# Two attention heads per step, W_out chunk by chunk with the router work between, and a slot table that a permutation turns

## The chip, the cores and the metric

One core of one Trainium2 chip. The core has five engines with queues of their own: TensorE (PE in the profile; PEld is its weight load), VectorE (DVE), ScalarE (ACT), GpSimd (POOL) and SyncE (SP), which here only issues transfers. The metric is the device time of one execution in microseconds (us). All times below are from the kernel before.

## The reference, cut to what matters

One layer of an encoder on 512 tokens of width 1024, all in fp32:

```
P    = h @ W_in                        # q, k, v of A, B, C and three gates
A    = windowed attention, 8 heads of 64, 2 kv heads, band of 128, ALiBi, sink logit
B    = differential attention, 4 heads, each softmax1 - lambda*softmax2, RMS norm
C    = 2-D neighbourhood attention, 8 heads of 64, relative bias
mix  = W_out( sum_i sigmoid(gate_i) * (branch_i @ W_branch_i) )
x    = LN(alpha*x + mix)
x    = LN(alpha*x + MoE(x))            # top-4 of 32 experts, clamped SwiGLU, softmax router
```

## The kernel before

Tokens lie in four chunks of 128. A product that has to be exact to fp32 is made of three in a faster form: a weight is split into a high part (a rounded copy by ScalarE) and a low part (VectorE subtracts), and the products are hi·hi, lo·hi and hi·lo. Rows such as L129 to L131 (projections) or L783 to L785 (W_out) are such triples.

*Attention* (until about 480 us). `scores` (L198) makes the scores of one head u and one block of 128 queries with two products: L203 takes all 128 rows of the array (the head's 64 channels with high and low part of the query stacked), L204 takes 64 rows (high query by low key), rows 0 to 63 for u = 0 and 64 to 127 for u = 1. They are evicted to VectorE's `soft` (L207; the reduction is L210), with two PSUM buffers `sc`. `banded` (L230; A and C) does one head after the other: four query blocks, then per key block transposes, a split of the transposed probabilities (ph, pl) and `pv3`, three products with 64 output columns (L226 vh·ph, L227 vl·ph, L228 vh·pl). `evac_o` (L273) writes the head's output as high and low part. Between the steps a filler (`Fill.run`) puts the projections of the next heads and the branch gates, so that the triples L129 to L131 stand between attention's products. The scheduler of the framework then settles each engine's order.

*Gates of the third branch* (480 to 546 us), a pure run of products. *W_out with LN1 and the router* (546 to 643 us): `out_product` for chunks 0 to 2 together, k by k as the eight blocks of W_out arrive; then `layer_norm1` for each, which makes the router's logits, the top four (mx, mf) and the mask M; then the products of chunk 3 with the three layer_norm1 on the other engines; then chunk 3's. After that the counts per expert (L816, L818), each token's place in its expert (pos, L821, L822), the first expert's rows by one-hot products (L835, eight per chunk, 64 instructions in the profile), `finish1` for the four chunks (L767, L768, writes of X1 and Y), `sort` of the experts by load.

*MoE* (643 us to the end): 32 experts in an order in which expert 0 is always first (it needs no `order`) and the rest are sorted by load; KINDS says which place is large (L, split weights, 128 slots) or small (S, plain fp32). A weight block is 1 MB; 8 up and 4 down blocks per expert. Eight raw buffers (rawu, rawv) hold the stream; SyncE asks for a block (L610 up, L615 down) when its buffer is free. The slot table T in DRAM, whose column is the expert's place in the order, is filled by 16 indirect DMAs of GpSimd (L933, one per chunk and top-k rank), read back by three (L938, L939) and gives the rows to gather (tbs, tbl). `pick` (L1019, a GpSimd copy) spreads an expert's column of the sorted selector for the bias product L1095. The up products are L1084 (large) and L1102 (small), the bias of a large expert is L1079 (64 rows, alternating row halves).

Of the kernel before, what the change touches and what calls it, by code (L numbers as in the profile page):

```python
# [43 lines left out]
def kernel_body(ctx, tc, a, out, dbg=None, cap=128):  # L44
# [56 lines left out]
    for k in range(8):  # L101
        t = att.tile([P, NB, P], F32, name="E", bufs=7) if k < 7 else att.tile([P, NB, P], F32, name="t", bufs=3)
# [66 lines left out]
    def make_v(w, permuted, box):  # L169
# [8 lines left out]
        vh = att.tile([P, NB, P], F32R, name="vh", bufs=2)  # L178
        vl = att.tile([P, NB, P], F32R, name="vl", bufs=2)
# [3 lines left out]
        nc.scalar.copy(vh, pt)  # L183
        nc.vector.tensor_sub(vl, pt, vh.bitcast(F32))
        box["v"] = (vh, vl)
# [12 lines left out]
    def scores(box, u, qb, ks, ke):  # L198
        q2, (k2, kl) = box["q"], box["k"]
        r = slice(u * 64, u * 64 + 64)  # L200
        qs = slice(qb * P, qb * P + P)
        ps = ps_s.tile([P, S], F32, name="sc")
        nc.tensor.matmul(ps[:, :ke - ks], q2[:, u, qs], k2[:, u, ks:ke], start=True, stop=False)  # L203
        nc.tensor.matmul(ps[:, :ke - ks], q2[r, u, qs], kl[r, ks:ke], start=False, stop=True)  # L204
        return ps[:, :ke - ks]

    def soft(ps, bias, n, init, mcol, scol):  # L207
# [3 lines left out]
        e = att.tile([P, S], F32, name="E", bufs=7)  # L211
# [18 lines left out]
    def banded(box, u, biasf, init, sinkc, done):  # L230
        vh, vl = box["v"]
        vc = slice(u * 64, u * 64 + 64)
        m = att.tile([P, NB], F32, name="m", bufs=4)
        s = att.tile([P, NB], F32, name="s", bufs=4)
        es = []
        for qb in range(NB):
            ks, ke = rng(qb)
            ps = scores(box, u, qb, ks, ke)
            es.append(soft(ps, biasf(qb), ke - ks, init, m[:, qb:qb + 1], s[:, qb:qb + 1]))
            yield  # L240
        if sinkc is not None:
            sk = att.tile([P, NB], F32, name="sk", bufs=2)
            nc.scalar.activation(sk, m, AF.Exp, bias=sinkc)
            nc.vector.tensor_add(s, s, sk)
        r = att.tile([P, NB], F32, name="r", bufs=4)
        nc.vector.reciprocal(r, s)
        for qb in range(NB):
            ks, ke = rng(qb)
            nc.vector.tensor_scalar(es[qb][:, :ke - ks], es[qb][:, :ke - ks], r[:, qb:qb + 1], None,
                                    op0=ALU.mult)  # L250
        yield
        po = ps_o.tile([P, S], F32, name="o")
        pend = None
        for i, kb in enumerate((1, 2, 0, 3)):
            qs = [qb for qb in range(NB) if abs(qb - kb) <= 1]
            pt = ps_t.tile([P, S], F32, name="pt")
            n = len(qs) * P
            for j, qb in enumerate(qs):
                c0 = kb * P - rng(qb)[0]
                nc.tensor.transpose(pt[:, j * P:(j + 1) * P], es[qb][:, c0:c0 + P], ident)  # L260
            ph, pl = split_pt(pt, n)
            if pend:
                pv3(*pend)
            pend = (po[:64, qs[0] * P:qs[0] * P + n], n, ph, pl, vh[:, kb, vc], vl[:, kb, vc], i == 0, i == 3)
            yield
        pv3(*pend)
        done(po[:64])
        yield
# [4 lines left out]
    def evac_o(po, br, half, permuted):  # L273
        bh, bl = br
        r = slice(half * 64, half * 64 + 64)
        hi, hf, lo, src = bh[r], bh[r].bitcast(F32), bl[r], po
        if permuted:
            hi, hf, lo = perm(hi), perm(hf), perm(lo)
            src = out4(src)
        if half == 0:  # L280
            nc.scalar.copy(hi, src)
            nc.vector.tensor_sub(lo, src, hf)
        else:
            t = att.tile([P, S], F32, name="w", bufs=4)
            tt = out4(t[r]) if permuted else t[r]
            nc.scalar.copy(tt, src)
            nc.scalar.copy(hi, tt)
            nc.vector.tensor_sub(lo, tt, hf)
# [10 lines left out]
    def att_a(p, box):  # L299
        for u in range(2):  # L300
            h = p + 4 * u
            bt = att.tile([P, 896], F32, name="bias", bufs=2)
            (dma if p == 0 else nc.scalar.dma_start)(bt[:, :384], abv[:, h])

            def bf(qb):
                o = 128 if qb == 0 else 0
                ks, ke = rng(qb)
                return bt[:, o:o + ke - ks]
            yield from banded(box, u, bf, nsink[:, h:h + 1], sink[:, h:h + 1],
                              lambda po: evac_o(po, br_of(brA, h // 2), h % 2, False))  # L310

    def att_b(h, box):
        bt = att.tile([P, 896], F32, name="bias", bufs=2)
        nc.scalar.dma_start(bt, btv[:, h])
        vh, vl = box["v"]
# [10 lines left out]
        for qb in range(NB):  # L326
# [3 lines left out]
            ee = []  # L330
            for u in range(2):
                ps = scores(box, u, qb, 0, S)
                ee.append(soft(ps, bt[:, o:o + S], S, BIG, m[:, u:u + 1], s[:, u:u + 1]))
# [8 lines left out]
        for kb in range(NB):  # L342
# [6 lines left out]
            pend = (po, S, ph, pl, vh[:, kb], vl[:, kb], kb == 0, kb == 3)  # L349
# [30 lines left out]
    def att_c(p, box):  # L380
# [23 lines left out]
    def ph2_items(i, brs, db):  # L404
# [12 lines left out]
        def load():  # L417
# [4 lines left out]
            if pre_hook and db % 2:  # L422
                pre_hook[0](last[0])
# [32 lines left out]
    def qkv(kind, i):  # L456
        box = boxes.setdefault((kind, i), {})
        if kind == "A":
# [6 lines left out]
                (win(o + 1024 + i * P), lambda w: make_v(w, pm, box), 5.6)]  # L465
# [45 lines left out]
    T = dram.tile([P * E, 2], I32, name="T")  # L511
# [76 lines left out]
    wsp[0] = sW.enter_context(tc.tile_pool(name="wsp", bufs=2))  # L588
    nraw = [0]
# [9 lines left out]
    experts = {0: slice(0, 1)}  # L599

    def expert(p):

        if p not in experts:
            experts[p] = bass.ds(nc.values_load(order[0:1, p:p + 1], engines=[mybir.EngineType.SP], min_val=0,
                                                max_val=E - 1), 1)
        return experts[p]

    def up_raw(p, k):
        raw = raw_tile()
        dma(raw, a["w_up"][expert(p), k * P:(k + 1) * P, :].rearrange("o p c -> (o p) c"))  # L610
        return raw

    def down_raw(p, t):
        raw = raw_tile()
        dma(raw.rearrange("p (k d) -> p k d", k=2),  # L615
            a["w_down"][expert(p), t * 256:(t + 1) * 256, :].rearrange("o (k p) d -> p (o k) d", p=P))
# [10 lines left out]

    pre_hook.append(lambda ins: prefetch(ins, NRA))
    fill.add([ph2_items(2, brC, db) for db in range(8)])
    while fill.cur or fill.loaded or fill.items:  # L630
# [18 lines left out]
    nc.gpsimd.iota(iota, pattern=[[1, P]], base=0, channel_multiplier=0, allow_small_or_imprecise_dtypes=True)  # L649
    gt = moe.tile([3 * E, NB, P], F32R, name="gt")  # L650
    id16 = moe.tile([P, P], F16, name="id16")
    nc.gpsimd.tensor_copy(id16, ident)
# [10 lines left out]
    nc.gpsimd.iota(pcol, pattern=[[0, 1]], base=0, channel_multiplier=1, allow_small_or_imprecise_dtypes=True)  # L663
    half = moe.tile([P, 1], F32, name="half")
    nc.gpsimd.tensor_scalar(half, pcol, 64.0, None, op0=ALU.is_ge)
    iot2 = moe.tile([P, 2, 64], F32, name="iot2")
    nc.gpsimd.iota(iot2, pattern=[[0, 2], [1, 64]], base=1, channel_multiplier=0,
                   allow_small_or_imprecise_dtypes=True)
    rop = moe.tile([E, E], F32, name="rop")
    kw = dict(channel_multiplier=0, allow_small_or_imprecise_dtypes=True)  # L670
    ranks = dict(L=0, S=NL)
    for p, kind in enumerate(KINDS):
        nc.gpsimd.memset(rop[:, p:p + 1], float(ranks[kind]))
        ranks[kind] += 1
    sel0 = moe.tile([P, 1], F32R, name="sel0")
    for i in range(4):
        nc.gpsimd.tensor_copy(sel0[i * E:(i + 1) * E], ident[0:E, 0:1])
    sel = moe.tile([P, 2, E], F32R, name="sel")
    nc.gpsimd.memset(sel.bitcast(F32), 0.0)
    bu = moe.tile([P, 2, S], F32R, name="bu")  # L680

    s3 = ExitStack()
    sO = ExitStack()
    po_ = sO.enter_context(tc.tile_pool(name="wout", bufs=1))
    wo = [po_.tile([P, 2, D], F32R, name=f"wo{k}") for k in reversed(range(8))][::-1]
# [3 lines left out]
    ps_r = s3.enter_context(tc.tile_pool(name="ps_r", bufs=2, space=PSUM))  # L689
    burs = []  # L690
    for i in range(2):
        bur = p3a.tile([P, 2, S], F32, name="xt", bufs=2)
        nc.scalar.dma_start(bur[:E], a["b_up"].rearrange("e (b n c) -> e n b c", b=2, n=2)[:, i])
        burs.append(bur)
# [7 lines left out]
    bonr = p3.tile([P, E], F32, name="bonr")  # L702
    nc.gpsimd.iota(bonr, pattern=[[-1, E]], base=E - 1, **kw)
    nc.gpsimd.memset(bonr[:, 0:1], 2.0 ** 17)
    bonc = p3.tile([E, 1], F32, name="bonc")
    bonj = p3.tile([E, E], F32, name="bonj")
    nc.vector.scalar_tensor_tensor(bonj, bonr[:E], 1.0, ident[:E, :E], ALU.mult, ALU.mult, bonc)
# [792 lines left out]
```

## Time and profile before

| | us |
|---|---|
| median of 3 runs | 1747.69 (1742.06 to 1747.76) |
| the profiled execution, its own time | 1744.16 |
| its span, first to last instruction | 1742.3 |
| busy: TensorE, VectorE, ScalarE, GpSimd | 1611.0, 940.0, 778.3, 207.1 |

A row of a timeline gives the start and the length of an instruction; since TensorE works on several at once, what one takes from the stream is the start of the next less its own start, not its length. A row of a waits view names who waited, for whom, the total, the number of times and the longest. In the stretches the columns after the engines are the granted share of TensorE's clock, the share of the DMA engines and the GB/s.

### The profile page before, as it was taken

The page shows a single profiled execution, that of the slowest core. Times are in us where ns is not written, and L with a number is a line of the kernel's source. Part 1 is how long each engine was busy: PE and PEld are TensorE (multiplying, and loading weights), DVE is VectorE, ACT ScalarE, POOL GpSimd, SP SyncE. Part 2 cuts the span into 40 slices and gives each one's busy share as a digit, 9 for nine tenths or more (in the row PEclk, how much of TensorE's full clock was granted, in tenths as well). Part 3 has the DMA queues.
Part 4 walks back from the last instruction along what each step waited for, and adds up shares of the span by engine and source line. Part 5 has one row for each costly group of instructions (what it writes and reads, how often), then busy time and mean ns, then how long its engine had stood idle before and what let it go on. Part 6 is the DMA issues. An engine that isn't in the chain of part 4 may idle for free.

```text
span 1742.3 us, 19860 instructions
## 1 busy us (share of the span) xinstructions
PE 1611.0 (92%) x7130; PEld 1053.7 (60%) x7130; DVE 940.0 (54%) x1340; ACT 778.3 (45%) x994; POOL 207.1 (12%) x247
## 2 busy tenths in 40 slices
PE   7999999999996966999899999999999999999994
PEld 5677777777785753455375466556546654664541
DVE  4875566555643375355274377536536753664424
ACT  4654545444432342345154266535535653453432
POOL 0000011212101016101012000110100011101000
PEclk9999999999998988999999999999999999999998
DMA  8212222222254164999899999999999999999994
GB/s 200 60 50 66 83 78 77 73 69 76 61 162 161 41 242 185 408 412 401 335 409 411 403 403 385 391 392 410 402 399 395 369 382 394 403 403 406 396 402 193
DMA packets 169208, 478.64 MB, mean 275 GB/s; under 512 B 24441, under 2 KB 94105, under 8 KB 136336
## 3 DMA queue, kind: packets, MB, share of 16 engines
q1 hardware_dynamic: 153648, 452.95, 66.9%
q0 software_dynamic: 8432, 16.21, 3.7%
q10 hardware_dynamic: 7024, 8.16, 1.6%
q8 instruction: 58, 0.95, 0.2%
q14 instruction: 46, 0.38, 0.1%
HBM read 466.78 MB, written 18.40 MB: 278 GB/s over the span
## 4 chain that ended last, share of the span: by engine, by line
PE 38%; DMA 5%; DVE 4%; ACT 3%; issue 1%; DVEq 0%; ACTq 0%
PE h L1084 15%; PE h L1102 7%; PE d L1151 7%; PE d L1166 6%; DVE wlo L1065 3%; DMA rawv<-in_w_down_dram 2%; ACT whi L1064 2%; DMA rawu<-in_w_down_dram 2%; DMA rawv<-in_w_up_dram 1%; PE x L1135 1%; PE x L1014 1%; PE h L1095 0%; ACT yoL L1181 0%; PE h L1079 0%; DVE whi L1413 0%
## 5 line engine op out<-in xcount | busy, mean ns | idle before, releaser
L1065 DVE TENSOR_TENSOR wlo<-rawv,whi 128x2048 fp32r<-128x2048 f32 x104 | 235.1, 2288 | 53.3 <-ACT whi L1064 41.6
L1084 PE MATMUL h<-whi,t 128*128 128x512 f32 x960 | 246.6, 399 | 9.0 <-ACT whi L1064 8.1
L1065 DVE TENSOR_TENSOR wlo<-rawu,whi 128x2048 fp32r<-128x2048 f32 x88 | 199.3, 2288 | 60.5 <-ACT whi L1064 60.1
L1064 ACT CAST whi<-rawv 128x2048 fp32r<-128x2048 f32 x104 | 197.0, 1912 | 55.0 <-DMA rawv<-in_w_down_dram 18.5
L1084 PEld LDWEIGHTS h<-whi,t 128*128 128x128 f32 x960 | 181.3, 190 | 57.3 <-ACT whi L1064 14.9
L1064 ACT CAST whi<-rawu 128x2048 fp32r<-128x2048 f32 x88 | 165.8, 1909 | 37.2 <-DMA rawu<-in_w_up_dram 17.1
L129 PE MATMUL mm<-xh,whi 128*128 128x512 f32 x432 | 178.0, 412 | 0.0
L130 PE MATMUL mm<-xl,whi 128*128 128x512 f32 x432 | 171.8, 398 | 0.0
L131 PE MATMUL mm<-xh,wlo 128*128 128x512 f32 x432 | 171.7, 397 | 0.0
L1114 ACT ACTIVATE sg<-h 128x512 f32<-128x512 f32 x48 | 28.7, 597 | 272.7 <-PE h L1102 152.2
L1151 PE MATMUL d<-whi,t 128*128 128x512 f32 x512 | 143.1, 401 | 2.9 <-ACT whi L1064 2.9
L1084 PE MATMUL h<-wlo,t 128*128 128x512 f32 x480 | 134.8, 402 | 2.2 <-DVE wlo L1065 2.1
L1102 PE MATMUL h<-rawu,xs 128*64 128x512 f32 x512 | 118.6, 603 | 3.6 <-DMA rawu<-in_w_up_dram 3.5
L1102 PE MATMUL h<-rawv,xs 128*64 128x512 f32 x512 | 117.8, 606 | 2.4 <-DMA rawv<-in_w_up_dram 2.4
L71 DVE TENSOR_TENSOR wlo<-raw,whi 128x1024 fp32r<-128x1024 f32 (+1 forms) x78 | 86.2, 1107 | 53.1 <-ACT whi L70 52.5
L1151 PEld LDWEIGHTS d<-whi,t 128*128 128x128 f32 x512 | 96.2, 191 | 27.1 <-ACT whi L1064 4.3
L1115 DVE TENSOR_SCALAR aS<-h 128x512 f32<-128x512 f32 x16 | 11.0, 690 | 187.3 <-PE h L1102 187.3
L1084 PEld LDWEIGHTS h<-wlo,t 128*128 128x128 f32 x480 | 88.9, 190 | 37.4 <-issue 9.7
L70 ACT CAST whi<-raw 128x1024 fp32r<-128x1024 f32 (+1 forms) x78 | 71.3, 915 | 77.2 <-PE mm L130 33.5
L1151 PE MATMUL d<-wlo,t 128*128 128x512 f32 x256 | 84.3, 411 | 14.8 <-DVE wlo L1065 14.7
L129 PEld LDWEIGHTS mm<-xh,whi 128*128 128x128 f32 x432 | 82.3, 190 | 23.0 <-issue 7.6
L212 ACT ACTIVATE E<-t,m 128x256 f32<-128x256 f32 (+2 forms) x96 | 59.1, 616 | 76.5 <-DVE m L210 71.8
(345 smaller groups left out, 2287.7 us busy)
## 6 DMA issues: line engine op xcount, KB each, us to landing
rawu<-in_w_up_dram SPq DMA_DIRECT2D x128, 1024.0 KB, 15.1
rawv<-in_w_up_dram SPq DMA_DIRECT2D x128, 1024.0 KB, 15.7
rawu<-in_w_down_dram SPq DMA_DIRECT2D x64, 1024.0 KB, 15.0
rawv<-in_w_down_dram SPq DMA_DIRECT2D x64, 1024.0 KB, 14.0
raw<-in_w_in_dram SPq DMA_DIRECT2D x50, 512.0 KB, 3.9
raw<-in_w_branch_dram SPq DMA_DIRECT2D x24, 256.0 KB, 2.8
raw<-in_w_out_dram SPq DMA_DIRECT2D x8, 512.0 KB, 5.8
raw<-in_w_in_dram SPq DMA_DIRECT2D x8, 256.0 KB, 4.7
```

Of the source, the lines that this page charges most:

```text
L70: nc.scalar.copy(h, raw)
L71: nc.vector.tensor_sub(l, raw, h.bitcast(F32))
L129: nc.tensor.matmul(ps, wv[0][:, k], xh[:, k], start=(k == 0), stop=False)
L130: nc.tensor.matmul(ps, wv[0][:, k], xl[:, k], start=False, stop=False)
L131: nc.tensor.matmul(ps, wv[1][:, k], xh[:, k], start=False, stop=(k == 7))
L212: nc.scalar.activation(e[:, :n], t[:, :n], AF.Exp, bias=mcol, scale=-1.0, accum_out=scol)
L1064: nc.scalar.copy(h, raw)
L1065: nc.vector.tensor_sub(l, raw, h.bitcast(F32))
L1084: nc.tensor.matmul(hs[n], x_[:, k], w_[:, n // 2, n % 2 * S:(n % 2 + 1) * S], start=False, stop=(last and k == 7))
L1102: nc.tensor.matmul(hs[b][n * 64:(n + 1) * 64], x_, w[:, b, n * S:(n + 1) * S], start=False, stop=(k == 7), skip_group_check=True)
L1151: nc.tensor.matmul(ys[n], x_[:, k], w_[:, j, n * S:(n + 1) * S], start=(k == 0 and i == 0), stop=(k == 7 and i == 2))
L1166: nc.tensor.matmul(ys[m * 64:(m + 1) * 64], x_, w[:, j, n * S:(n + 1) * S], start=(k == 0), stop=(k == 7), skip_group_check=True)
```

## The change

Attention. `scores` makes both heads of a block in one call: first the two full products, then the two of 64 rows. The value tile holds high and low part side by side, so that banded attention's three products become two: one with 128 output columns (v hi and lo by ph) and one with 64 (vh·pl). `evac_o` has to add the two halves.

```
+        pss = [ps_s.tile([P, S], F32, name="sc")[:, :ke - ks] for _ in range(2)]
+        for u in range(2):
+            nc.tensor.matmul(pss[u], q2[:, u, qs], k2[:, u, ks:ke], start=True, stop=False)
+        for u in range(2):
+            r = slice(u * 64, u * 64 + 64)
+            nc.tensor.matmul(pss[u], q2[r, u, qs], kl[r, ks:ke], start=False, stop=True)
...
+                nc.tensor.matmul(po[:, cs], v2[:, kb, u], ph[:, :n], start=first, stop=False, skip_group_check=True)
+                nc.tensor.matmul(po[:64, cs], v2[:, kb, u, :64], pl[:, :n], start=False, stop=last,
...
+        t = att.tile([P, S], F32, name="w", bufs=4)
+        nc.scalar.copy(t[r], po[64:])
+        nc.vector.tensor_add(t[r], po[:64], t[r])
...
+        nc.scalar.copy(hi, src)
+        nc.vector.tensor_sub(lo, src, hf)
```

W_out. Two W_out blocks are asked for during the last gates, three more at their end. The chunks go one after the other, and chunk c's work of LN1, router, position and one-hot product is cut into stages that are emitted between the products of chunk c + 1. The constants of GpSimd are made after the fifth block's split (`setup`), x, LN1's and the bias's loads go from ScalarE's queue to SyncE's. Counts and sorting are split up, and stand before the first expert. `rawB`, the second half of the weight buffers, is still opened after the last product.

```
+    for c in range(NB):
+        pss[c] = [ps_y.tile([P, S], F32, name="y") for _ in range(2)]
...
+            out_product(c, k)
+            if k in (1, 2, 4, 5, 7):
+                stage()
+            if c == NB - 1 and k == 6:
+                stage()
+                gates(range(NB - 1))
...
+    with tc.issue_after(chain["dve"].ins):
+        table_at(c)
+        gates([c])
+        rest_of_sort()
        finish1(c)
```

The table. A slot is now expert times 128 plus position, which needs no sorting: the first 12 indirect DMAs are emitted with chunk 3's products, the last four after the first expert's rows. One DMA reads the table back, six small products with the permutation (L1070, L1072 of the changed kernel) turn it into the experts' order, inside expert 0's up products.

```
+        nc.gpsimd.dma_start(tt, T.rearrange("(e s) i -> e s i", s=P))
...
+        for j, t in ((0, tf), (1, tt[:, :, 1].bitcast(F32))):
+            nc.tensor.matmul(pt[:, j], t, perm_, start=True, stop=True, skip_group_check=True)
+            for i in range(2):
+                nc.tensor.matmul(pt[i * 64:(i + 1) * 64, 2 + j], t[:, :64], perm_, start=True, stop=True,
+                                 skip_group_check=True)
...
-        for i in range(2):
-            nc.gpsimd.dma_start(tbs[i * 64:(i + 1) * 64], tv[:64])
-        nc.gpsimd.dma_start(tbl, tv)
```

What the scheduler makes of it, at three places: attention C, attention A and the start of expert 1. TensorE in attention C before (sc is a score buffer, L129 to L131 a projection, L182 transposes of v):

```order
L131 MATMUL mm_3006<-xh_80,wlo_2867 128x512
L203 MATMUL sc_3078<-k2_2592,q2_2520 128x256
L204 MATMUL sc_3078<-kl_2593,q2_2520 128x256
L203 MATMUL sc_3091<-k2_2592,q2_2520 128x384
L204 MATMUL sc_3091<-kl_2593,q2_2520 128x384
L203 MATMUL sc_3104<-k2_2592,q2_2520 128x384
L182 MATMUL mm_3062<-ident_60,w_3058 128x128 x4
L129 MATMUL mm_3069<-xh_80,whi_2925 128x512
L130 MATMUL mm_3069<-xl_81,whi_2925 128x512
```

and after, where L208 and L211 are the full and the 64-row product:

```order
L129 MATMUL mm_2915<-xh_80,whi_2843 128x512
L130 MATMUL mm_2915<-xl_81,whi_2843 128x512
L131 MATMUL mm_2915<-xh_80,wlo_2844 128x512
L208 MATMUL sc_2954<-k2_2571,q2_2502 128x256
L208 MATMUL sc_2955<-k2_2571,q2_2502 128x256
L211 MATMUL sc_2954<-kl_2572,q2_2502 128x256
L211 MATMUL sc_2955<-kl_2572,q2_2502 128x256
L129 MATMUL mm_2984<-xh_80,whi_2849 128x512
```

The two 64-row products of a step now stand side by side. They do so in all 16 steps of C and in 12 of the 16 of B. In attention A they don't; TensorE there after the change:

```order
L208 MATMUL sc_318<-k2_229,q2_297 128x256
L211 MATMUL sc_318<-kl_230,q2_297 128x256
L208 MATMUL sc_345<-k2_229,q2_297 128x384
L211 MATMUL sc_345<-kl_230,q2_297 128x384
L130 MATMUL mm_334<-xl_81,whi_330 128x512
L131 MATMUL mm_334<-xh_80,wlo_331 128x512
L208 MATMUL sc_346<-k2_229,q2_297 128x384
L211 MATMUL sc_346<-kl_230,q2_297 128x384
L129 MATMUL mm_334<-xh_80,whi_330 128x512
L208 MATMUL sc_359<-k2_229,q2_297 128x384
```

Each full product is still followed by its own 64-row product, as before. TensorE between expert 0 and expert 1, before (h is an accumulator of up products; pick_5809 belongs to expert 1, pick_5886 to expert 2):

```order
L1084 MATMUL h_5573<-wlo_5759,xt0_5456 128x512
L1004 MATMUL x_5802<-ident_60,xg1_5800 128x128 x4
L1095 MATMUL h_5891<-bu_4936,pick_5809 128x512
L1095 MATMUL h_5892<-bu_4936,pick_5809 128x512
L1095 MATMUL h_6059<-bu_4936,pick_5886 128x512
L1102 MATMUL h_5891<-rawu_5811,xs_5807 64x512 x2
L1102 MATMUL h_5892<-rawu_5811,xs_5807 64x512 x2
```

and after (pick_5796 of expert 1, pick_5873 of expert 2):

```order
L1201 MATMUL h_5649<-wlo_5746,xt0_4870 128x512
L1212 MATMUL h_5878<-bu_4869,pick_5796 128x512
L1219 MATMUL h_5878<-rawu_5798,xs_5794 64x512
L1212 MATMUL h_5879<-bu_4869,pick_5796 128x512
L1219 MATMUL h_5878<-rawu_5798,xs_5794 64x512
L1219 MATMUL h_5879<-rawu_5798,xs_5794 64x512 x2
...
L1212 MATMUL h_6046<-bu_4869,pick_5873 128x512
```

The bias product of expert 2 stood ahead of all products of expert 1; it now stands behind them, at its own expert. GpSimd at the same place, before:

```order
L909 CAST sel_4934<-perm_5545 32x32 x4
L1021 CAST pick_5809<-sel_4934 128x128
L933 DMA T_305<-row_5638,di_5637 4096x2 x16
L990 MEMSET xgS_5884 128x512
L1021 CAST pick_5886<-sel_4934 128x128
```

and after:

```order
L748 MEMSET sel_4868 128x64
L883 DMA T_304<-row_4858,di_4861 4096x2 x12
L1162 CAST pick_5796<-sel_4868 128x128
L883 DMA T_304<-row_4858,di_4861 4096x2 x4
L1064 DMA tt_5694<-T_304 32x256
L1131 MEMSET xgS_5871 128x512
L1162 CAST pick_5873<-sel_4868 128x128
```

The copy for expert 2 still stands behind the indirect DMAs, but 12 of the 16 now stand ahead of expert 1's copy, and the read-back is one transfer.

## Rows read from the trace of the kernel before

**Rows 1.** Stretches: us; busy us (x instructions) by engine, TensorE clock, DMA share, GB/s
```profile
core 0 of [0], span 1742.3 us
...
40.00:120.00 80.00, 79.91 (x380) 54.79 (x379) 64.59 (x182) 52.91 (x138) 1.22 (x2) 1.00 0.22 64
140.00:480.00 340.00, 334.08 (x1498) 251.78 (x1497) 195.21 (x374) 162.25 (x309) 54.40 (x61) 1.00 0.25 73
...
691.00:1740.00 1049.00, 979.86 (x4243) 578.02 (x4239) 539.66 (x409) 466.78 (x398) 112.87 (x95) 0.98 0.98 388
```

**Rows 2.** TensorE by start time, attention B: start us, us, instruction (rows 3 to 5 too)
```profile
222.93 0.39 PE L203 MATMUL sc<-k,q 128*128 128x512 f32 x1
223.25 0.50 PE L204 MATMUL sc<-kl,q 64*128 64x512 f32 x1
223.68 0.50 PE L129 MATMUL mm<-xh,whi 128*128 128x512 f32 x1
224.01 0.39 PE L130 MATMUL mm<-xl,whi 128*128 128x512 f32 x1
```

**Rows 3.** TensorE by start time, attention C, scores
```profile
334.39 0.28 PE L203 MATMUL sc<-k,q 128*128 128x256 f32 x1
334.60 0.38 PE L204 MATMUL sc<-kl,q 64*128 64x256 f32 x1
334.91 0.45 PE L203 MATMUL sc<-k,q 128*128 128x384 f32 x1
```

**Rows 4.** TensorE by start time, attention C, a value product chain
```profile
332.43 0.39 PE L131 MATMUL mm<-xh,wlo 128*128 128x512 f32 x1
332.66 0.28 PE L226 MATMUL o<-ph,vh 128*64 128x256 f32 x1
...
332.89 0.28 PE L228 MATMUL o<-pl,vh 128*64 128x256 f32 x1
333.01 0.39 PE L129 MATMUL mm<-xh,whi 128*128 128x512 f32 x1
```

**Rows 5.** TensorE by start time, bias products of an expert
```profile
887.06 0.73 PE L1079 MATMUL h<-bu,sel 64*128 64x512 f32 x4
887.72 0.50 PE L1084 MATMUL h<-whi,t 128*128 128x512 f32 x1
```

**Rows 6.** VectorE lines, attention: shapes and count, busy us, mean ns, idle before
```profile
L210 DVE CUSTOM_DVE_ANT_0 t<-sc,bias 128x512 f32<-128x512 f32 x32 | 21.7, 683 | 11.3 <-PE sc L204 11.1
...
L288 DVE TENSOR_TENSOR brl<-w,brh 64x512 fp32r<-64x512 f32 x7 | 4.8, 688 | 2.9 <-ACT brh L287 2.8
```

**Rows 7.** TensorE by start time, from the last gate to expert 1
```profile
545.41 0.39 PE L434 MATMUL mm<-brh,wlo 128*128 128x512 f32 x1
...
557.53 0.77 PE L783 MATMUL y<-wo,mx 128*128 128x512 f32 x1 [11.73 <-ACT wo L793]
...
613.75 0.40 PE L785 MATMUL y<-wo,mx 128*128 128x512 f32 x1
...
628.36 9.61 PE L835 MATMUL y<-oh,mx 128*128 128x128 f32 x64 [0.83 <-DVE oh L833]
...
643.24 2.07 PE L1084 MATMUL h<-whi,xt 128*128 128x512 f32 x4
...
687.50 1.12 PE L1102 MATMUL h<-rawu,xs 128*64 128x512 f32 x2
```

**Rows 8.** VectorE by start time, two of eight like pieces after the output products
```profile
615.05 2.35 DVE L767 TENSOR_TENSOR mx<-mx,ln 128x1024 f32<-128x1024 f32 x2
```

**Rows 9.** What TensorE waited for, 520 to 760 us: total, times, longest
```profile
PE h L1095 <- POOL pick L1021: 13.3, 1, 13.3
```

**Rows 10.** GpSimd by start time, slot table
```profile
663.93 2.87 POOL L933 DMA_INDIRECT T<-row,di  x1 [13.66 <-DVE di L925]
...
686.40 0.31 POOL L1021 CAST pick<-sel 128x128 fp32r<-128x128 f32 x1
```

**Rows 11.** SyncE's queue: first weights asked for after the gap
```profile
691.21 0.39 SPq L615 DMA_DIRECT2D rawu<-in_w_down_dram  x1
```

More of the change, by code (lines that the diff above doesn't have):

```diff
@@ L247, in banded @@
[L247 to L264, printed above, removed]
+            pss = scores(box, qb, ks, ke)
@@ new lines, in kernel_body, with stage, behind @@
+    x_load(0)
+    queue = []
+    def stage():
+        if queue and next(queue[0], "end") == "end":
+            queue.pop(0)
+            stage()
+    def behind(c, mid=None):
+        yield from layer_norm1(c, pss[c], mid)
+        rows = first_rows(c)
+        next(rows)
+        yield
+        next(rows)
+        if c < NB - 1:
+            table_at(c)
+            finish1(c)
+        yield
+    for c in range(NB):
+        pss[c] = [ps_y.tile([P, S], F32, name="y") for _ in range(2)]
+        zs[c], x1s[c] = (None, None)
+        for k in range(8):
+            if c == 0:
+                if k > 4:
+                    out_raw(k, *((wraw,) if k < 7 else (po_,)), **(dict(bufs=3) if k == 7 else {}))
+                nc.scalar.copy(wo[k][:, 0], wos[k])
+                nc.vector.tensor_sub(wo[k][:, 1], wos[k], wo[k][:, 0].bitcast(F32))
+                if k == 4:
+                    g_ = nc.gpsimd.tensor_copy(gate0, wo[4][0:1, 1, 0:1].bitcast(F32))
+                    with tc.issue_after(g_.ins):
+                        setup()
+            out_product(c, k)
+            if k in (1, 2, 4, 5, 7):
+                stage()
+            if c == NB - 1 and k == 6:
+                stage()
+                gates(range(NB - 1))
+                nc.scalar.activation(warm, gk[:, NB - 2, 0:1], AF.Sqrt)
+        if c == 0:
+            bu_load()
+            for i, n_ in enumerate(("ln1_g", "ln1_b")):
+                dma(ln1[:, i], bcast(a[n_], D))
+            x_load(1)
@@ new lines, in chunks, with ready @@
+    def chunks():
+        for p in range(E + 1):
+            if p < E:
+                for k in range(8):
+                    yield KINDS[p], (p == 0 and pre.get(("u", k))) or up_raw(p, k)
+            if p:
+                for t in range(4):
+                    yield KINDS[p - 1], (p == 1 and pre.get(("d", t))) or down_raw(p - 1, t)
+    stream, ahead = chunks(), deque()
+    def ready():
+        kind, raw = next(stream, ("", None))
+        if raw is None:
+            return False
+        raw = raw.rearrange("p (j c) -> p j c", j=2)
+        if kind == "L":
+            h, l = (ring.tile([P, 2, D], F32R, name=n) for n in ("whi", "wlo"))
+            with ExitStack() as order_:
+                for e in chain.values():
+                    order_.enter_context(tc.issue_after(e.ins))
+                nc.scalar.copy(h, raw)
+                nc.vector.tensor_sub(l, raw, h.bitcast(F32))
+            raw = h, l
+        ahead.append((kind, raw))
+        return True
@@ L845, in kernel_body, with ready_first @@
+    def ready_first(held):
+        chain.clear()
+        chain["dve"] = held
+        ready()
+    last_ = behind(c, ready_first)
+    next(last_)
+    while queue:
+        stage()
+    for _ in range(3):
+        next(last_)
+    counts()
+    next(last_)
+    sort()
     for q in range(2):
         s4 = slice(q * 4, q * 4 + 4)
-        chain["act"] = nc.scalar.copy(xt0[:, s4, 0], x32[:, s4])
-        chain["dve"] = nc.vector.tensor_sub(xt0[:, s4, 1], x32[:, s4], xt0[:, s4, 0].bitcast(F32))
```

546 lines of the change are left out of this document (282 added, 264 removed).

## The prediction

> **What bounds the kernel now.** I read the table of stretches first [rows 1]. From 40 to 120 us (attention A) and from 140 to 480 us (B, C and the gates between them) TensorE is busy 79.9 of 80 and 334.1 of 340 us at full clock; VectorE has 64.6 of 80 in A, and well under 60% later. So a product that disappears there is time, as long as VectorE doesn't take over, and A is where it could. From 691 us to the end the DMA engines are busy to 0.98 and move 388 GB/s: the MoE is the weight stream, and it ends a fixed time after the stream has restarted. I then looked up that restart in SyncE's queue: the first request after a gap is at 691.21 [rows 11], 3.7 us after TensorE's first product of expert 1 at 687.50 [rows 7], which frees the buffers that the request waits for. From there to the end of the span it is 1742.3 - 691.2 = 1051 us. Nothing of the change touches the blocks of that stream, so what counts is how early expert 1 starts. Third, TensorE by start time between the gates and expert 1 gives four marks [rows 7]: last gate product 545.41 (its stream ends 0.23 later, 545.64), first output product 557.53, last 613.75 (ends 613.98), first product of expert 0 643.24, first of expert 1 687.50. That is 68.3, 29.3 and 44.3 us. Last, the waits: one of 13.3 us, for a copy on GpSimd [rows 9].
>
> **Attention: scores.** What a product takes is the step to the next start. In B [rows 2]: the full product 0.32, the 64-row product 0.43, the product behind it 0.33. A plain one of 512 columns takes 0.23 (332.43 to 332.66) [rows 4]. So going to 64 rows and back costs 0.09 + 0.20 + 0.10 = 0.39 us. Two heads apart are 2 x (0.32 + 0.43 + 0.10) = 1.70. With the 64-row products side by side, run together: 0.23 + 0.32 + 0.43 + 0.10 = 1.08, a saving of 0.62; run one behind the other, 0.23 more, a saving of 0.39. For 256 columns [rows 3], of which one streams in 0.12 [rows 4]: 2 x (0.21 + 0.31 + 0.10) = 1.24 against 0.12 + 0.21 + 0.31 + 0.10 = 0.74, saving 0.50 or 0.38. For 384 I take the mean, 0.56. That opposite row halves run together this trace shows: four bias products in alternating halves take 0.66 us with entry and exit [rows 5], where four in a row would be 0.92. The order gives pairs in 12 steps of B and 16 of C, none in A: 12 x 0.62 + 8 x 0.56 + 8 x 0.50 = 15.9 us. The other end, all pairs serial: 28 x 0.385 = 10.8. In A the scores save nothing.
>
> **Attention: values.** One of three products per key block goes: 0.12 for 256 columns [rows 4], 0.17 for 384 (between 0.12 and 0.23), two of each per head, 0.58 a head, 4.6 us for the 8 heads of C and 4.6 for those of A. In C VectorE has room. In A it gets an extra pass of 64x512 per head, like L288's 688 ns [rows 6]: 8 x 0.69 = 5.5, so 70.1 us in some 75. That nearly full I credit 3 of the 4.6 (ends 0 and 4.6). Attention in all: 15.9 + 4.6 + 3.0 = 23.5; ends 10.8 + 2 + 0 = 13 and 25.
>
> The Trainium skill, in "TensorEngine Tiling (Array Packing)", section Tiling Modes, says under Key Properties that changing the tiling mode drains TensorE. For 64 rows the trace agrees, with the 0.39 above. For 64 columns it doesn't: the step into them is 0.23 and the step out 0.12, both plain [rows 4]. By the rule the change, which goes from 128 to 64 columns in every key block, would pay there too; that is rival C.
>
> **W_out.** The wait of 11.7 us before its first product [rows 7] was for a block to arrive and be split. Two blocks are now asked for during the gates; a split's worth, some 4 us, stays. The 192 products are 192 x 0.23 = 44 us either way. The other 12 us between 557.53 and 613.98 (transposes, logits, stalls for blocks) I put at 8, and three quarters of the one-hot products, 0.75 x 9.61 = 7.2 us, come in from behind. 4 + 44 + 8 + 7 = 63 to 64 against 68.3: a gain of 4.3. Ends: -3, if chunk 0 alone can't cover the arrival of the blocks, and 8. The loads moved to SyncE's queue are eight requests of 0.4 us each, going by the row of such a request [rows 11]; 3 us in a queue that is idle in chunks 1 to 3. GpSimd's constants lie beside chunk 0's products; without that cover they would cost their few us once.
>
> **To expert 0.** In the 29.3 us stood eight VectorE pieces of `finish1`, 2.35 us a pair, 9.4 us, between the pieces of chunk 3's router chain [rows 8], and 9.6 us of one-hot products [rows 7]. Six of the eight and three quarters of the products move ahead of the last output product, the rest of the pieces behind the first expert's rows. 29.3 - 9.4 - 7.2 = 12.7, say 13: a gain of 16.3 (ends 8 and 19). What is late next is chunk 3's own chain through LN1, top four and positions.
>
> **To expert 1.** TensorE waited 13.3 us [rows 9] since the bias product of expert 2 stood ahead of expert 1's products, and its copy on GpSimd behind 16 indirect DMAs, from 663.93 to 686.40, 1.4 us each [rows 10]. In the order that bias product now stands behind expert 1. That removes the 13.3. In its place comes a new wait: the turning products L1070 stand in expert 0's sixth block, and TensorE holds all of expert 0's remaining products behind them until the table is read back. The other 31 us for eight blocks are 3.9 each, so it gets there 33 us after the last output product (13 + 20). The last four indirect DMAs start, by my estimate, 18 us after it (13 and the slot arithmetic of chunk 3), take 4 x 1.4 = 6 us, and the landing and the read-back come on top, which no row shows by itself; with 6 to 12 us for these the table is there at 30 to 36. I take a wait of 4; ends 0 and 17. So 44.3 - 13.3 + 4 = 35, a gain of 9.3 (ends -4 and 13.3).
>
> **Sum.** 4.3 + 16.3 + 9.3 = 29.9 us earlier restart of the stream, after 23.5 from attention: 53.4. The profiled execution took 1744.16; 1744.2 - 53.4 = 1690.8. The median of the runs lies 3.5 us above it, so I forecast 1694. Not all ends fall together: 13 + 15 gives 1720, 25 + 40 gives 1683.
>
> **Rivals.**
> A. The table's read-back is late by its upper end. TensorE takes instructions in order, so all 17 us go to expert 1's start: 1694 + 13 = 1707, and with a slow chain of chunk 3 (8 instead of 16) 1715. For it: the indirect DMAs are 1.4 us each and the last four wait for chunk 3. Against: 12 are issued early.
> B. The pairs run one behind the other and A gains nothing: 10.8 + 4.6 = 15.4 instead of 23.5, 1702. Rows 5 speak against.
> C. A 64-column product costs entry and exit like a 64-row one: 64 key blocks x 0.39 = 25 us, 1719. Rows 4 speak against.
> D. Slower. One step now takes both score buffers, so TensorE can't start the next pair before VectorE has read both, 2 x 0.68 and the reading of the accumulators, 1.5 us [rows 6]. If nothing else stood between, 44 steps (28 pairs and A's 16) would wait 1.5 each, 66 us: 1694 + 66 = 1760. It decides from 53.4 / 44 = 1.2 us a step. Against: VectorE waited 11.3 us for scores in those 32 evictions, not TensorE for VectorE [rows 6], and the order has a dozen projection products, 3 us, between most pairs.
> E. The weights' stream is held elsewhere, so that an earlier expert 1 is given back: the 29.9 is lost, 1724. The gap before 691.21 and the 0.98 after it [rows 1, 11] speak against.
>
> **Chances.** Forecast (1680 to 1703) 0.50, A 0.16, B 0.10, C 0.06, D 0.07, E 0.07, rest faster than 1680 0.04. Range 1678 to 1721: it leaves out D, E and the few fastest, under 2 in 10. For the forecast alone 1682 to 1704. Within 0.5% (8.7 us, about what can be told from no change) lie only D where it is mild and a pair of the others together, 0.04; slower, D in full, 0.05; faster 0.91.
>
> **What would show it.** Score pairs in C: two L211 starting together, and 1.0 us or less for a step of four products. Value products: no step longer than 0.23. The gates should end about 23 us earlier, at 522; the first output product 4 us after them, the last 64 after; expert 0's first product 13 behind that, expert 1's 48 behind. A wait of L1070 for a VectorE copy of the read table, of 0 to 17 us, replaces the one for GpSimd's copy. From expert 1's start to the end it should be 1055 us as before, at 0.98 DMA share. I am wrong if TensorE shows waits on L210 in attention, if A's VectorE is at 100% with TensorE idle, or if the restart comes early and the end doesn't.

## The result: 1719.97 us, 1.4% faster, half of what was forecast

Four runs of the changed kernel gave a median of 1719.97 us (1716.42 to 1722.20), those of the kernel before beside them 1746.88. The ratio is 0.9856, with a 95% interval of 0.9838 to 0.9874. The forecast was 1694 and its range 1678 to 1721, so the time lies at the slow end of the range. The medians differ by 26.9 us, the two profiled executions, which the marks below are taken from, by 22.8.

The stretches of the changed kernel, with the columns of [rows 1]:

```profile
core 0 of [0], span 1719.6 us
...
40.00:120.00 80.00, 76.44 (x342) 52.44 (x340) 64.79 (x175) 53.32 (x136) 2.13 (x2) 0.96 0.18 55
140.00:470.00 330.00, 319.37 (x1459) 248.44 (x1458) 194.25 (x384) 162.79 (x311) 54.67 (x61) 0.98 0.26 74
664.70:1717.00 1052.30, 985.79 (x4252) 580.38 (x4251) 542.88 (x420) 467.16 (x400) 106.50 (x95) 0.98 0.98 386
```

TensorE has lost full occupation and full clock in attention (76.4 of 80 us at 0.96; 319.4 of 330 at 0.98), where it was all but full [rows 1]. The MoE is as it was. The five marks of [rows 7], on TensorE after the change (L445 last gate product, L835 and L837 first and last output product, L1201 expert 0, L1219 expert 1):

```profile
539.30 0.39 PE L445 MATMUL mm<-brh,wlo 128*128 128x512 f32 x1
543.19 0.47 PE L835 MATMUL y<-wo,mx 128*128 128x512 f32 x1 [3.50 <-DMA ln<-in_ln_g_dram]
...
605.29 0.39 PE L837 MATMUL y<-wo,mx 128*128 128x512 f32 x1
...
621.35 3.11 PE L1201 MATMUL h<-whi,xt 128*128 128x512 f32 x8
...
664.72 0.64 PE L1219 MATMUL h<-rawu,xs 128*64 128x512 f32 x1
```

| stage | before | after | gain | forecast gain |
|---|---|---|---|---|
| start to end of the gates | 545.6 | 539.5 | 6.1 | 23.5 |
| gates to last output product | 68.3 | 66.0 | 2.3 | 4.3 |
| last output product to expert 0 | 29.3 | 15.8 | 13.4 | 16.3 |
| expert 0 to expert 1 | 44.3 | 43.4 | 0.9 | 9.3 |
| expert 1 to the end of the span | 1054.8 | 1054.9 | 0 | 0 |
| sum | 1742.3 | 1719.6 | 22.7 | 53.4 |

So two terms failed: attention, by 17 us, and the way from expert 0 to expert 1, by 8. The products themselves did get shorter. A pair of 256 columns in C:

```profile
321.89 0.40 PE L208 MATMUL sc<-k,q 128*128 128x256 f32 x2
322.22 0.38 PE L211 MATMUL sc<-kl,q 64*128 64x256 f32 x2
322.53 0.49 PE L129 MATMUL mm<-xh,whi 128*128 128x512 f32 x1
```

Four products take 322.53 - 321.89 = 0.64 us, and the two of 64 rows together 0.31, as one did [rows 3]. What came instead is in the same step 5 us later. TensorE:

```profile
326.90 0.48 PE L129 MATMUL mm<-xh,whi 128*128 128x512 f32 x1
329.54 0.33 PE L275 MATMUL pt<-ident,E 128*128 128x128 f32 x1 [2.16 <-DVE E L258]
```

It waits 2.16 us for VectorE's scaling of E (the exponentials of a block of scores, divided by their sum before they are transposed). VectorE:

```profile
325.69 1.05 DVE L258 TENSOR_SCALAR E<-E,r 128x256 f32<-128x256 f32 x2
328.36 0.69 DVE L165 TENSOR_TENSOR kl<-mm,k 64x512 fp32r<-64x512 f32 x1 [1.62 <-ACT k L164]
329.07 2.88 DVE L258 TENSOR_SCALAR E<-E,r 128x384 f32<-128x384 f32 x5
```

Between two of the eight scalings stands the low part of a key (L165), which waits for ScalarE. ScalarE (ACTq is its queue asking for a transfer):

```profile
327.37 0.33 ACTq L401 DMA_DIRECT2D craw<-in_na_rpb_dram  x1
327.75 0.58 ACT L164 CAST k<-mm 64x512 fp32r<-64x512 f32 x1 [3.36 <-POOL bias L404]
```

Its cast of that key stood behind a request for the raw bias `craw`, and the request waited for GpSimd, which had to read the one buffer of `craw` empty first. GpSimd:

```profile
323.15 2.70 POOL L404 TENSOR_TENSOR bias<-cm,craw 128x256 f32<-128x256 f32 x2 [17.10 <-DVE m L217]
```

It had been idle for 17 us, up to VectorE's last reading of the scores (L217), since the two bias tiles are now both in use until both heads' scores are done; before, the first was free a head earlier. Four queues stand in a row. The same stop is there at 376.4 and 424.9 us. And behind it TensorE works at a lower clock; the columns of [rows 1] for three stretches of the changed kernel, behind the stop before B's second score (for POOL's copy of a key, 1.78 us), behind the one above, and behind the wait for the table (between expert 0 and expert 1, see e2 below):

```profile
107.90:114.90 7.00, 6.77 (x19) 4.36 (x20) 6.05 (x17) 3.31 (x7) 0.00 (x0) 0.52 0.42 127
329.50:333.40 3.90, 3.86 (x14) 3.02 (x14) 3.27 (x6) 0.88 (x2) 2.62 (x3) 0.56 0.01 2
646.70:654.20 7.50, 7.50 (x26) 5.99 (x27) 6.75 (x23) 0.00 (x0) 0.00 (x0) 0.50 0.57 209
```

That is the lower of the two levels, 1.2 GHz, in each of them; below it is called half clock. In attention the trace before had one such stretch, of 6.8 us at 121 us, which the changed kernel has as well; the one at 107.9 and all those in C are new. Between expert 0 and expert 1 the kernel before had one too, from 677.4 to 691.0 us, but TensorE stood idle there until 686.8, so that only some 4 us of its work fell into it.

### The profile page after: what moved, and what is told of

Its sections match the earlier page's. It is cut to its first block, busy times and chain, and to the rows that moved or that the text cites. A ratio compares the mean times of both kernels' runs of the same rounds, so it can differ in the third digit from the quotient of the medians.

```text
span 1719.6 us, 19754 instructions
## 1 busy us (share of the span) xinstructions
PE 1602.4 (93%) x7078; PEld 1053.3 (61%) x7078; DVE 940.4 (55%) x1313; ACT 785.8 (46%) x1009; POOL 200.5 (12%) x243
## 4 chain that ended last, share of the span: by engine, by line
PE 38%; DVE 5%; ACT 4%; DMA 4%; issue 1%; DVEq 0%; SPq 0%; ACTq 0%
PE h L1201 15%; PE d L1268 8%; PE h L1219 7%; PE d L1283 6%; DVE wlo L1004 3%; ACT whi L1003 3%; DMA rawv<-in_w_down_dram 2%; DMA rawu<-in_w_down_dram 2%; PE x L1252 1%; PE x L1155 1%; ACT yoL L1298 1%; PE h L1212 0%; PE h L1196 0%; DVE whi L1532 0%; PE x L1406 0%
## 5 line engine op out<-in xcount | busy, mean ns | idle before, releaser
L1201 PE MATMUL h<-whi,t 128*128 128x512 f32 x960 | 250.1, 403 | 9.6 <-ACT whi L1003 8.3
L1201 PEld LDWEIGHTS h<-whi,t 128*128 128x128 f32 x960 | 182.7, 192 | 60.7 <-ACT whi L1003 17.0
L1003 ACT CAST whi<-rawu 128x2048 fp32r<-128x2048 f32 x88 | 165.3, 1907 | 34.8 <-DMA rawu<-in_w_up_dram 15.8
L129 PE MATMUL mm<-xh,whi 128*128 128x512 f32 x432 | 177.3, 410 | 0.0
L130 PE MATMUL mm<-xl,whi 128*128 128x512 f32 x432 | 172.8, 400 | 0.0
L131 PE MATMUL mm<-xh,wlo 128*128 128x512 f32 x432 | 172.7, 400 | 0.0
L1201 PE MATMUL h<-wlo,t 128*128 128x512 f32 x480 | 134.7, 402 | 2.9 <-DVE wlo L1004 2.9
L71 DVE TENSOR_TENSOR wlo<-raw,whi 128x1024 fp32r<-128x1024 f32 (+1 forms) x78 | 85.8, 1100 | 68.3 <-ACT whi L70 67.1
L1219 PE MATMUL h<-rawu,xs 128*64 128x512 f32 x512 | 118.0, 596 | 3.3 <-DMA rawu<-in_w_up_dram 3.1
L1219 PE MATMUL h<-rawv,xs 128*64 128x512 f32 x512 | 116.1, 600 | 1.5 <-DMA rawv<-in_w_up_dram 1.5
L1201 PEld LDWEIGHTS h<-wlo,t 128*128 128x128 f32 x480 | 88.9, 189 | 38.0 <-issue 9.7
L129 PEld LDWEIGHTS mm<-xh,whi 128*128 128x128 f32 x432 | 82.6, 191 | 21.2 <-issue 5.7
L131 PEld LDWEIGHTS mm<-xh,wlo 128*128 128x128 f32 x432 | 82.4, 191 | 18.0 <-issue 0.6
## 6 DMA issues: line engine op xcount, KB each, us to landing
rawu<-in_w_down_dram SPq DMA_DIRECT2D x64, 1024.0 KB, 14.9
rawv<-in_w_down_dram SPq DMA_DIRECT2D x64, 1024.0 KB, 13.5
```

The lines of the kernel that those rows point to most:

```text
L71: nc.vector.tensor_sub(l, raw, h.bitcast(F32))
L129: nc.tensor.matmul(ps, wv[0][:, k], xh[:, k], start=(k == 0), stop=False)
L130: nc.tensor.matmul(ps, wv[0][:, k], xl[:, k], start=False, stop=False)
L131: nc.tensor.matmul(ps, wv[1][:, k], xh[:, k], start=False, stop=(k == 7))
L1003: nc.scalar.copy(h, raw)
L1201: nc.tensor.matmul(hs[n], x_[:, k], w_[:, n // 2, n % 2 * S:(n % 2 + 1) * S], start=False, stop=(last and k == 7))
```

## The experiments

Ratios are to the kernel before, run beside them. They ran in three groups, e1 to e4, e6 to e9, and e10 with e11, beside which the kernel before had medians of 1742.34, 1745.33 and 1743.59 us; a difference of 2 or 3 us between runs of two groups says little. The marks (when the gates end, when an expert starts) are read from TensorE's timeline of the one profiled execution, as above.

**The request on another queue (e1).**

```
-            nc.scalar.dma_start(raw, rp[h])
+            nc.gpsimd.dma_start(raw, rp[h])
```

> The changed kernel, with the load of attention C's raw bias asked for on GpSimd's queue instead of ScalarE's. Theory (stop by a queue): in C three stops of TensorE of 2.1 us each come from ScalarE, whose queue holds the request for the second head's raw bias until GpSimd has read the first one out of the single buffer; behind it stand the cast of k, VectorE's low part of k, the scaling of E and TensorE's transposes. Then the stops shrink below 1 us, the half-clock stretches after them (330.0, 377.8, 425.6 us) go, and the time falls by 8 to 11 us to about 1710. Rival (VectorE's clump): two heads' softmax at once make VectorE late by itself; the stops stay at 2 us and the time at 1720.

Measured: 1707.86 (1706.58 to 1708.51), 0.9797 (0.9780 to 0.9814). TensorE's waits for the scaling in C, in the changed kernel:

```profile
PE pt L275 <- DVE E L258: 6.5, 3, 2.2
```

and in e1:

```profile
PE pt L275 <- DVE E L258: 1.7, 3, 0.6
```

The whole of C, 300 to 470 us, the changed kernel and then e1 (columns as in [rows 1]):

```profile
300.00:470.00 170.00, 160.86 (x740) 126.26 (x739) 97.71 (x198) 81.03 (x168) 35.02 (x35) 0.96 0.24 71
```

```profile
300.00:470.00 170.00, 166.50 (x794) 131.50 (x794) 101.13 (x207) 85.91 (x176) 39.81 (x41) 1.00 0.28 82
```

5.6 us more of busy TensorE and full clock; the gates end at 527.0 instead of 539.5. The theory holds, the rival (VectorE late by itself) falls: the same work on VectorE, and the waits for the scaling fall from 6.5 to 1.7 us.

**Work in the stop (e4).** The changed kernel with:

```
+                if sinks is None and u == 0 and i == 0:
+                    for _ in range(16):
+                        nc.tensor.transpose(pt[:, 3 * P:], ident, ident)
```

> The changed kernel with 16 transposes of the identity into an unused quarter of the PSUM tile ahead of the first transposes of each step of C (1.7 us of TensorE work, four times, whose result nobody reads). Theory (the clock pays for the stop): they fill the three stops without lengthening the wait, the half-clock stretches behind them go, and the time falls by about 5 us (6.8 less the 1.7 in the step that has no stop). Rival: the clock falls for another reason, or the stop itself is all that counts: no change, or 2 to 7 us slower.

Measured: 1723.64 (1722.02 to 1728.68), 0.9899 (0.9877 to 0.9922), slower than the changed kernel. Its waits in C:

```profile
PE o L265 <- ACT ph L228: 3.9, 2, 2.1
PE o L266 <- DVE pl L229: 3.5, 5, 1.5
PE pt L278 <- DVE E L258: 1.9, 3, 0.7
```

The stop only moved on to the value products (L265, L266), behind ScalarE, which was still held; the half clock came with two of three such stops (1.8 and 2.1 us, not 1.5). So it doesn't test whether work in the stop would keep the clock up. It fits that the hold, not the place where TensorE meets it, costs the time.

**Attention as before (e3).** The changed kernel with the old `scores`, `banded`, `evac_o` and value tiles.

> The changed kernel with the attention of the kernel before (one head after the other, three value products, seven E buffers), everything else as changed. By the marks of the two traces attention brought 6 us, so 1726. By the sum of the prediction it would have brought 23.5, so 1743.

Measured: 1725.52 (1718.85 to 1727.66), 0.9888 (0.9861 to 0.9915): by the medians attention in two heads is worth 5.5 us as it stands. The runs of the two overlap, but in the profiles the gates end at 549.2 us in e3 and at 539.5 in the changed kernel.

**Pairs undone in the mended kernel (e10).** e8 below, with:

```
         for u in range(2):
             nc.tensor.matmul(pss[u], q2[:, u, qs], k2[:, u, ks:ke], start=True, stop=False)
-        for u in range(2):
             r = slice(u * 64, u * 64 + 64)
```

> The kernel of e8 with each head's two score products emitted together again, so that no two 64-row products of opposite halves stand side by side (28 pairs go); the rest as in e8. If pairs run together, as the prediction took it, attention ends 16 us later (28 pairs at 0.50 to 0.62 us) and the time is 1709 to 1713. If they ran one behind the other, 11 us later, 1704 to 1708. If stops in C eat the saving: under 5 us.

Measured: 1719.35 (1714.92 to 1722.83), 0.9866 (0.9843 to 0.9888). A pair of 256 columns in C, undone:

```profile
330.71 0.28 PE L208 MATMUL sc<-k,q 128*128 128x256 f32 x1
330.92 0.38 PE L210 MATMUL sc<-kl,q 64*128 64x256 f32 x1
331.23 0.38 PE L208 MATMUL sc<-k,q 128*128 128x256 f32 x1
331.55 0.38 PE L210 MATMUL sc<-kl,q 64*128 64x256 f32 x1
331.86 0.50 PE L129 MATMUL mm<-xh,whi 128*128 128x512 f32 x1
```

The four products take 331.86 - 330.71 = 1.15 us, where the pair took 0.64 in the changed kernel: 0.51 saved, as the prediction had it (0.50). The gates end at 541.9 against 527.1 in e8, 14.8 us later. Some 1.3 of it is not the pairs': e10 is late by that much at the first score of A, ahead of any pair, in e8 and then in e10:

```profile
39.14 0.36 PE L208 MATMUL sc<-k,q 128*128 128x256 f32 x1
40.47 0.36 PE L208 MATMUL sc<-k,q 128*128 128x256 f32 x1
```

At B's second score, behind the passage from A to B, it is late by 1.0 (143.59 against 142.64), so the 28 pairs are worth 13.5 to 13.8 us: between the 10.8 of serial pairs and the 15.9 of the prediction, and nearer to the latter. The 23 us of the medians are more than the marks give; in the profile itself the span is 19 longer, so some 4 come behind the gates.

**A's values in three products (e11).** e8 with the old three products and no added pass for A alone:

```
+                if sinks is not None:
+                    return pv3(po[:64, cs], n, ph, pl, v2[:, kb, u, :64], v2[:, kb, u, 64:], first, last)
```

> The kernel of e8 with attention A's value products in three again, and its outputs written without the added pass of VectorE (C keeps two). The prediction credited A with 3 us of 4.6. If that holds: 1699. If VectorE or the passage to B takes it all: 1695 to 1697, no difference. If the added pass costs more than the product saves: faster, 1692 to 1695.

Measured: 1691.81 (1690.61 to 1696.04), 0.9709 (0.9685 to 0.9733), the fastest of all. The intervals of e8 and e11 overlap; by the marks the gates end at 520.7, 6.4 us before e8's. The end of A, 100 to 120 us, in e8 and then in e11:

```profile
100.00:120.00 20.00, 15.29 (x69) 9.63 (x67) 17.21 (x41) 12.38 (x30) 0.00 (x0) 1.00 0.29 86
```

```profile
100.00:120.00 20.00, 19.54 (x106) 14.21 (x104) 17.93 (x45) 14.82 (x33) 0.00 (x0) 1.00 0.34 100
```

TensorE goes from 15.3 to 19.5 of 20 us, and in this stretch there are 5 of the projections' L130 in e8 and 12 in e11: with the merged products the filler has run out before the end of A, and A's last transposes and value products wait for VectorE and ScalarE with little between them. VectorE itself is not busier in e8 (17.2 against 17.9 us). Two things besides the products are in the 6.4: the half clock that e8 has from 121.3 to 128.1 us, some 3.4 us of loss, is not there in e11, and the scheduler made 30 score pairs in e11, not 28.

**The key's copy at the passage from A to B (e6).** e1 with ScalarE in place of GpSimd for attention B's first key (k2's other half).

> The kernel of e1 (raw bias on GpSimd's queue), with the copy of attention B's first key to the other row half made by ScalarE instead of GpSimd. At the passage from A to B TensorE stopped 1.8 us for that copy, and 7 to 10 us at half clock followed. Theory (stop and clock): the stop goes below 1 us, the half clock behind it goes, C's first score comes 3 to 6 us earlier and the time falls from 1708 to 1702 to 1705. Rival (the tail of A has no other work to give TensorE): the next wait in the chain of transposes, casts and subtractions takes its place, and the time is within 2 us of e1's.

Measured: 1711.51 (1708.08 to 1715.92), 0.9804 (0.9779 to 0.9830): no gain over e1. The wait for the key went, and one of 1.65 us for the scaling of E took its place, as the rival had it. Half clock followed in this profile, 27.3 us of it from 112 to 143 us; in that of e8, which has the same attention and the same wait, only 6.8 us of it came, at 121.

**The table's turn later (e2).** Changed kernel with `hs = up(0, {1: [sel_copies], 4: [second], 7: [table]})`, where sel_copies holds table's four copies.

> The changed kernel, with the six turning products of the slot table emitted after expert 0's eighth block instead of its second (the selector's copies stay). Theory: TensorE's wait of 9.2 us and the half clock after it (some 3.8 us) go, since the table is there at 646 us and these products would be reached at about 652; the weight stream restarts 10 to 13 us earlier and the time falls to 1707 to 1710. Rival: what is late is the gather for expert 2, which needs the table, so that the stop only moves behind expert 1: under 3 us gained.

Measured: 1719.67 (1716.61 to 1723.69), 0.9861 (0.9840 to 0.9883): nothing by the medians. In the profile expert 0 to expert 1 took 40.4 us instead of 43.4, and attention, which the edit doesn't touch, ended 6.2 us later. In the changed kernel TensorE waited so:

```profile
637.09 0.39 PE L1201 MATMUL h<-whi,xt 128*128 128x512 f32 x1
646.66 0.60 PE L1070 MATMUL x<-perm__4862,tf 32*128 32x32 f32 x2 [9.19 <-issue]
```

GpSimd's last four indirect DMAs and the read-back:

```profile
630.56 2.78 POOL L883 DMA_INDIRECT T<-row,di  x1 [2.58 <-DVE row L880]
...
638.03 0.98 POOL L883 DMA_INDIRECT T<-row,di  x1 [0.30 <-issue]
644.36 0.59 POOL L1064 DMA_DIRECT2D tt<-T  x1 [5.35 <-DMA T<-row,di]
```

and VectorE, which had the last steps of the router's gates (L879 and L880) between weight splits of 2.28 us:

```profile
627.92 2.28 DVE L1004 TENSOR_TENSOR wlo<-rawu,whi 128x2048 fp32r<-128x2048 f32 x1
630.12 0.16 DVE L880 COPY row<-gk 128x4 f32<-128x4 f32 x1
...
646.35 0.21 DVE L1067 CAST tf<-tt 32x128 f32<-32x128 int32 x1 [9.47 <-DMA tt<-T]
```

VectorE's copy of the table (L1067) itself stands for 9.47 us at the head of its queue. In e2 TensorE's products no longer wait for it, but that copy still stood in VectorE's queue ahead of the one-hots of expert 1's gather (L1175); VectorE, then TensorE of e2:

```profile
654.45 0.22 DVE L1069 CAST tf<-tt 32x128 f32<-32x128 int32 x1 [7.84 <-DMA tt<-T]
```

```profile
646.79 1.07 PE L1203 MATMUL h<-wlo,xt 128*128 128x512 f32 x4
655.27 1.12 PE L1175 MATMUL x<-mx,oh 128*64 128x512 f32 x2 [7.41 <-issue]
```

A wait of 7.4 us, at the next product that needs VectorE. The rival's size (under 3 us gained) fits the marks, but not its place: the stop is at expert 1's gather, not expert 2's.

**Both queues freed (e7).** e1 and e2, and the copy ordered behind the one-hots:

```
-        nc.vector.tensor_copy(tf, tt[:, :, 0])
+        with tc.issue_after(last["oh"].ins):
+            nc.vector.tensor_copy(tf, tt[:, :, 0])
```

> The kernel of e1, with the turning products behind expert 0's eighth block as in e2, and VectorE's copy of the read-back table ordered behind the one-hots of expert 1's gather, in front of which e2 had it. Theory (two in-order queues, TensorE's and VectorE's, stood behind the read-back): now neither does; expert 0's first product to expert 1's takes 33 to 36 us instead of 42.5, and the time falls to 1698 to 1702. Rival: expert 1's start is held by its own gather or its weights, and the time stays within 3 us of e1's.

Measured: 1699.01 (1695.51 to 1700.76), 0.9743 (0.9718 to 0.9767). What is left of the wait in e7:

```profile
PE x L1073 <- DVE tf L1070: 0.8, 1, 0.8
```

Expert 0 to expert 1 takes 639.65 - 608.32 = 31.3 us, against 42.5 in e1, and no half clock follows.

**All three (e8).**

> e6 and e7 together. If both theories hold and add up: 1693 to 1699, near the 1694 of the prediction. If only the table's does: 1698 to 1702.

Measured: 1696.11 (1695.77 to 1698.52), 0.9727 (0.9702 to 0.9752). Beside e7 that is no clear difference.

**A warm wait (e9).** The changed kernel with 110 transposes of the identity ahead of the turning products.

> The changed kernel with 110 transposes of the identity ahead of the turning products, 81 of them (some 9 us at full clock) right where TensorE waits 9.2 us for the table; their result is overwritten. Theory (the clock falls behind an idle stretch and costs after it): the wait is spent working, the half clock from 640.6 to 654.3 goes, and expert 1 starts some 4 us earlier: 1716, with the 29 others costing 1 to 3 us where they don't hide. Rival (the clock isn't bound to the idleness): no gain, 1720 to 1723.

Measured: 1723.32 (1722.78 to 1724.25), 0.9880 (0.9856 to 0.9905). It doesn't test the theory:

```profile
625.96 9.01 PE L1070 MATMUL x<-ident 128*128 128x128 f32 x81
641.33 0.63 PE L1072 MATMUL x<-perm__4862,tf 32*128 32x32 f32 x2 [6.37 <-DVE tf L1067]
```

The scheduler put the 81 transposes behind 24 of expert 0's 96 products, three weight blocks earlier than the changed kernel has the wait (behind 61), and those blocks behind the table. TensorE still idled 6.4 us, and the half clock came.

## Why the prediction was wrong, point by point

The range of 1678 to 1721 holds the time, but not by what was to fill it: the sum's slow end, 1720, stood for 13 us from attention and 15 from the restart of the stream, and they were 6.1 and 16.6. That rival C named 1719 is chance as well.

*Scores.* Right: pairs run together, 0.51 us saved by one of 256 columns and 13.5 to 13.8 by all (e10), for the 0.50 and 15.9 forecast.

*Values in C.* Not tested by themselves. *Values in A*, the 3 us of 4.6: they did not come. VectorE was seen to be nearly full, but the step took that as a discount; undoing it (e11) ends the gates 6.4 us earlier, some 3 without the half clock that went with it. What ran short was the filler at A's end, which the sum did not look at.

*What is late next in attention.* This is the step that failed most: "In C VectorE has room", and no cost for a stop. I asked whether VectorE had room in C and found that it had, by its busy share. I did not follow the two bias tiles: freed a head later by the new order, they hold GpSimd, GpSimd holds a request on ScalarE's queue, and this holds the casts. The first score of C, before, after the change and in e1:

```profile
288.17 0.36 PE L203 MATMUL sc<-k,q 128*128 128x256 f32 x1
285.33 0.36 PE L208 MATMUL sc<-k,q 128*128 128x256 f32 x1
284.44 0.36 PE L208 MATMUL sc<-k,q 128*128 128x256 f32 x1
```

From there to the end of the gates it is 257.5, 254.2 and 242.5 us. So C gained 3.3 us of the 13.1 forecast (8.5 for its pairs, 4.6 for its values), and 14.9 with the request moved: the hold cost 11.7 us, of which the waits are 4.8 (6.5 less 1.7) and the clock behind them 6.8, three half-clock stretches of 3.4, 6.8 and 3.4 us at half speed. Ahead of C the gain was 2.8 us instead of 10.4; an extra half-clock stretch of 6.8 us at the passage from A to B is 3.4 of that, and the 3 for A are most of the rest. With e8's and e11's edits attention ends 24.9 us earlier than before. That it is near the 23.5 of the sum is partly luck: 3 of these were for A's values, which e11 undoes, and 3.4 of the 24.9 come from the half clock at 121 us, which e11 doesn't have and the kernel before had.

*The clock.* No term of the sum held it. A stop on TensorE was priced as its own length.

*W_out.* The rest of the wait before its first product was put at 4 us and is 3.5 (its row names a load for LN1; in e2, e3 and e4 the same 3.5 us are put down to the block's split by ScalarE, as forecast); the products with what lies between them took 62.3 against 60.

*To expert 0.* 15.8 against 13; the three waits of chunk 3's chain that I named as late next are there, 1.1, 1.1 and 2.4 us, and half clock with them (609.9 to 623.5 us; in the kernel before at the same stage, 619.3 to 633.0).

*To expert 1.* The wait for GpSimd's copy went as the order showed. The wait that took its place was forecast at 4 (0 to 17) and was 9.2, and then another 7.5 us ran at half clock. Rival A, in part: the step that was mis-sized is the start of the last four indirect DMAs, put at 18 us after the last output product and measured at 630.56 - 605.52 = 25. The four took 8.5 us instead of 6; landing and read-back, put at 6 to 12, took from 639.0 to 646.4. So the table was there 41 us after the last output product, not 30 to 36. Without the waits (e7) expert 0 to expert 1 takes 31.3 us, the 31 of the sum.

*The stream.* Right: from expert 1 to the end 1054.9 against 1054.8.

*Rivals.* B's pairs run together; its other half, that A gains nothing, came true. C fell: value products after the change, L266 with 64 columns and L265 with 128, step at 0.12 us for 256 elements, in and out:

```profile
101.64 0.28 PE L266 MATMUL o<-pl,v 128*64 128x256 f32 x1
101.76 0.28 PE L265 MATMUL o<-ph,v 128*128 128x256 f32 x1
101.88 0.40 PE L129 MATMUL mm<-xh,whi 128*128 128x512 f32 x1
```

D, waits on score buffers, had the right thought, that a step of two heads holds two buffers, on the wrong buffers: the bias tiles, not the scores, for which TensorE waited 0.3 us in all of attention. E fell.

What stays open: whether the stop itself brings the clock down, since both experiments that were to fill a stop with work (e4, e9) missed it. Some stops of 1.6 to 1.8 us at the passage from A to B are followed by half clock (seven of the profiles, the changed kernel's among them) and others aren't at once (e7, e8), while all three of 2.1 us in C were; and the half clock of the kernel before at 121 us came with no wait of TensorE over 0.6 us in the 20 us ahead of it.

## What to carry to other kernels

When two units of work are merged into one step, list every buffer that the two used in turn and ask who refills it, on which queue, and what stands behind that request: a busy share of 60% on an engine says nothing on a hold that comes through another engine's queue. Price a stop on TensorE with the half clock that may follow it, not only by its length. A result read back from memory should be waited for neither by a product nor by a copy at the head of an in-order queue that still has other work; moving one of the two mostly moved the wait here (e2).

## What the runs showed of the hardware that was not expected

The half-clock stretches differ between executions with the same attention: behind the passage from A to B one of 6.8 us and another of 6.8 in the changed kernel's profile, a single one of 27.3 us in e2's, whose gates end 6.2 us later (545.7 against 539.5). The spread of the runs of the changed kernel may come from there: they stand in the order of the mean clock that each was granted, 1716.4 us at 0.979, 1718.6 at 0.975, 1721.3 at 0.972 and 1722.2 at 0.970. That the clock is the cause was not tested.
